# Experts' weights in transfers of 2 MB instead of 1 MB, into ten slots instead of twenty-one, with features and inner units in the order of the runs

## The chip, the core and the metric

The kernel runs on one core of one Trainium2 chip. The core has five engines: PE (TensorE, the matmuls; PEld is its loading of the stationary operand), DVE (VectorE), ACT (ScalarE), POOL (GpSimd) and SP (SyncE, which in this kernel only issues transfers), and 16 DMA engines that share its transfers out. The metric is the time of the whole kernel on the device, in microseconds (us), as the median of several runs.

## What is computed

The reference is one block of a diffusion transformer, for 256 latent tokens of 1024 features and 256 context tokens, in fp32. The first half (an adaLN-modulated norm, a combined projection, retention and latent attention side by side, a gated merge and an output projection) is not touched by the change. The second half is a mixture of 32 experts, of which each token gets four:

```python
h2 = modulate(rms_norm(x, norm2_g), m_lat[3], m_lat[4])
logits = h2 @ router_w + router_b                    # 32 experts
top_val, top_idx = lax.top_k(logits, 4)
gates = softmax(top_val)
...
gu = xb @ w_gu[e] + b_gu[e]                          # 1024 x 2048
gate, up = gu[:, :1024], gu[:, 1024:]
gate = minimum(gate, 7.0); up = clip(up, -7.0, 7.0)
glu = gate * sigmoid(1.702 * gate)
y = ((up + 1.0) * glu) @ w_down[e] + b_down[e]       # 1024 x 1024
...
x = x + m_lat[5] * sum over the token's experts of gate * y
out = rms_norm(x, final_norm_g)
```

An expert's weights are 8 MB (w_gu) and 4 MB (w_down), so that 32 experts are 402.7 MB (million bytes) that have to be read once. The sums over features (in w_gu) and over inner units (in w_down) may be taken in any order, as long as both factors of a product follow the same one.

## The kernel before

**The first half** is written as a list of steps (`step`), each with a weight that is loaded some steps ahead by SP (`load`, L258, tiles `w_...`), split into two parts by ACT (L267) and DVE (L268), and multiplied in three passes on PE (L276 to L278). It ends with the output projection (`w_out`, eight loads of 512 KB), the residual, and the transposes of the new x for the router (`x2_rows`, through the helper at L147).

**The experts** run one after the other, two sharing one gather. A block of up to 64 tokens per expert is enough for these inputs, and the code for more tokens (`overflow`) is branched over. For each expert PE does:

- the biases, `gu_bias` (L1307), once per expert, which begin the banks of the first layer
- `gate_up` (L1444): eight blocks k of 128 features; the stationary operand is xg, the gathered, transposed tokens (128 features x 64 slots), the moving one the weights, 512 columns at a time. In its middle stands `combine` (L1426), which adds the expert before to its tokens
- on DVE and ACT the clamps and the gating (L1448 to L1452), which end in `up`: 64 slots on each half of the partitions, 512 inner units each
- `slot_rows` (L1415) and `gather` (L1393) for the experts to come: 24 matmuls per expert, whose stationary operands are 128 features of the tokens in three bfloat16 parts (tiles `acc_m` and `x`)
- `hidden`: four transposes of `up` (L147), ACT copies them to hT
- `down` (L1473): eight blocks f of 128 inner units, hT stationary and the weights moving. `weigh` follows on DVE and ACT. The last expert's is done by columns (L1595), so that the last norm can begin earlier.

**The weights** come in 384 transfers of 1 MB, all issued by SP, in the order of their use: per expert eight by `load_gu` (L1067: 128 rows of 2048, a row of 8 KB to each partition), then four by `load_down` (L1072: rows p and p + 128 of 256, two runs of 4 KB to a partition). The very last one is issued in two halves (`load_last`). They go to a ring of 21 slots of 8 KB per partition. The slots come into being as the first half gives back its memory: `add_ring` opens some, with one load each. `open_first` has 2, which are reserved from the start, `RINGS = 4, 3, 9, 1` the others, and two more take the place of the output projection's operands (`halves`). From then on a slot is loaded again when PE has done its last matmul on it. SP works its transfers off in order, at most eight of them in flight.

Of the kernel before, what the change touches and what calls it, by code (L numbers as in the profile page):

```python
# [20 lines left out]
T = 256  # L21
# [8 lines left out]
RINGS = 4, 3, 9, 1  # L30
# [29 lines left out]
def hybrid_block(ctx: ExitStack, tc: tile.TileContext, A, out, dbg=None):  # L60
# [27 lines left out]
    first = [enter(ctx, f"first{i}", side="right", reuse_waits="tile") for i in range(2)]  # L88
# [12 lines left out]
    crow = sp.tile([16, 128], F32, name="crow")  # L101
    grow = sp.tile([21, 128], F32, name="grow")
# [9 lines left out]
    nc.gpsimd.dma_start(grow[8:16], A["norm2_g"].rearrange("o (k p) -> (o k) p", p=128))  # L112
    nc.gpsimd.dma_start(grow[16:19], A["mla_q_norm_g"].rearrange("o (k p) -> (o k) p", p=128))
    nc.gpsimd.dma_start(grow[19:21], A["mla_kv_norm_g"].rearrange("o (k p) -> (o k) p", p=128))
# [34 lines left out]
    def rsqrt(p, ss, n, mul, name="rs_y"):  # L149
        """(ss * mul + EPS) ** -0.5"""  # L150
# [34 lines left out]
    g1c, g2c, qgc, kvgc = cols[:, 0:8], cols[:, 8:16], cols[:, 16:19], cols[:, 19:21]  # L185

    def gain_cols():
        rp = pt_()
        transpose(rp[:, 0:21], grow)
        nc.vector.tensor_copy(cols, rp[:, 0:21])  # L190

    # ada[32 g + r]: (shift, scale) of columns 0.., then 512..; then gate, gate, shift, shift; scale, scale, gate, gate
# [4 lines left out]
    # The work up to the output projection is a list of steps; those with weights get them loaded and split ahead.  # L197
# [6 lines left out]
    def run_steps():  # L204
# [40 lines left out]
    def load(src, r0, nk, pieces, raw=False):  # L245
        """rows r0.. (nk blocks of 128), the columns of all pieces side by side"""
# [72 lines left out]
    def ada_step(q, k):  # L319
        """columns 2048 (q + 1).. of the modulation, rows 128 k.."""  # L320
# [59 lines left out]
    def project(pieces, jobs, kks, mid=None, at=None):  # L380
        """jobs: (bank, part of it, token tile, first column, end column of the loaded ones, starts its bank)"""
# [20 lines left out]
    def matmul2(names, wname, r0, c0, src, k0, first, last):  # L402
        """256 rows from r0 of a weight matrix, 512 columns, against the blocks k0.. of transposed tokens"""
# [195 lines left out]
    def q_up(quad, kks):  # L599
        """queries of four heads: the transposed parts without positions, and the rotated ones"""  # L600
# [42 lines left out]
    def q_rot(pair):  # L643
        """the rotated parts: the high parts in the upper 64 rows, what they lack in the lower"""
# [34 lines left out]
    def scores(pair):  # L679
        """softmax of both heads, for both token tiles"""  # L680
# [83 lines left out]
    def log_decay():  # L764
        """log_sigmoid(r) = min(r, 0) - log1p(exp(-|r|)), log1p(e) = 2 atanh(e / (2 + e))"""
# [41 lines left out]
    def open_ret():  # L807
# [13 lines left out]
        # the normed tokens as rows, in the two parts  # L821
# [14 lines left out]
    def r_rows():  # L836
        """the normed, gated output of a head, transposed and split"""
# [110 lines left out]
    # scores against the normed tokens first, then the value columns of w_in  # L948
# [33 lines left out]
    def gate_ret_out(c):  # L982
        """the heads so far and the other branch, gated; the gate stays for the last head"""
# [10 lines left out]
    for h in range(RH):  # L994
# [25 lines left out]
        if h == RH - 1:  # L1020
            step(lambda: open_first())
# [43 lines left out]
    def load_gu(wgu, k):  # L1065
        w = wtile()
        nc.sync.dma_start(w, wgu[128 * k:128 * k + 128])  # L1067
        return w

    def load_down(wdn, j):  # L1070
        w = wtile()
        nc.sync.dma_start(w.rearrange("p (r n) -> p r n", r=2),  # L1072
                          wdn[256 * j:256 * j + 256].rearrange("(r p) n -> p r n", p=128))
        return w

    def load_last(wdn, j):
        w = wtile()
        for r in range(2):
            nc.sync.dma_start(w[:, 1024 * r:1024 * r + 1024], wdn[256 * j + 128 * r:256 * j + 128 * r + 128])
        return w  # L1080
# [3 lines left out]
            for f, name, n in ((load_gu, "exp_w_gu", 8), (load_down, "exp_w_down", 4)) for i in range(n)]  # L1084
    todo[-1] = load_last, *todo[-1][1:]
# [5 lines left out]
    def take(f, src, i):  # L1091
        """the next weights of the experts in their order, or others"""
# [584 lines left out]
```

## Time and profile before

| what | before |
|---|---|
| time, 3 runs | 1523.48, 1525.47, 1526.0 us; median 1525.47 us |
| profiled execution, first to last instruction | 1526.6 us |
| busy: PE, PEld, DVE, ACT | 94%, 50%, 40%, 23% |
| mean granted TensorE clock | 0.991 of full |
| bytes that DMA moved | 492.42 MB, mean 323 GB/s |
| first matmul on an expert's weights | 582.27 us |
| first such matmul of the last expert | 1481.86 us |

The profile is of one execution, and it comes as a page and as views of its trace. In the page's rows of 40 slices each number stands for 38.2 us. A group of instructions is a row: line, engine, operation, tiles written and read, count, then busy time and mean ns of one, then the idle time of the engine before them and what ended it. In a timeline the first number is the start in us, the second how long the stretch took, and the brackets hold the idle time before it and its cause. In the windows view each stretch has its length, the busy time (and instructions) of PE, PEld, DVE, ACT and POOL, the granted clock, the mean busy share of the 16 DMA engines (it can pass 1 a little, since packets at the edges are counted whole) and GB/s.

### The profile page before, as it was taken

The page shows a single profiled execution, that of the slowest core. Times are in us where ns is not written, and L with a number is a line of the kernel's source. Part 1 is how long each engine was busy: PE and PEld are TensorE (multiplying, and loading weights), DVE is VectorE, ACT ScalarE, POOL GpSimd, SP SyncE. Part 2 cuts the span into 40 slices and gives each one's busy share as a digit, 9 for nine tenths or more (in the row PEclk, how much of TensorE's full clock was granted, in tenths as well). Part 3 has the DMA queues.
Part 4 walks back from the last instruction along what each step waited for, and adds up shares of the span by engine and source line. Part 5 has one row for each costly group of instructions (what it writes and reads, how often), then busy time and mean ns, then how long its engine had stood idle before and what let it go on. Part 6 is the DMA issues. An engine that isn't in the chain of part 4 may idle for free.

```text
span 1526.6 us, 19528 instructions
## 1 busy us (share of the span) xinstructions
PE 1427.5 (94%) x7977; PEld 761.8 (50%) x7977; DVE 614.0 (40%) x1079; ACT 345.9 (23%) x606; POOL 77.6 (5%) x98
## 2 busy tenths in 40 slices
PE   8999999999999998999999998899898889898985
PEld 4676787888888774333333333333332333233323
DVE  4486645556476573332322332222322232223223
ACT  4354533444344341010110101100110011001001
POOL 3100040101010020000000000000000000000000
PEclk9999999999999999999999999999999999999998
DMA  8635364354548877999999999999999999999994
GB/s 314 200 108 169 135 207 134 111 173 130 170 120 287 314 288 282 415 415 418 416 415 417 416 417 415 416 418 417 415 417 416 417 415 418 417 415 416 417 417 183
DMA packets 117658, 492.42 MB, mean 323 GB/s; under 512 B 9488, under 2 KB 19789, under 8 KB 84793
## 3 DMA queue, kind: packets, MB, share of 16 engines
q1 hardware_dynamic: 116616, 489.23, 82.1%
q0 software_dynamic: 544, 1.21, 0.3%
q8 instruction: 64, 1.05, 0.3%
q10 hardware_dynamic: 400, 0.66, 0.1%
q14 instruction: 34, 0.27, 0.0%
HBM read 490.02 MB, written 1.05 MB: 322 GB/s over the span
## 4 chain that ended last, share of the span: by engine, by line
PE 61%; DMA 29%; DVE 7%; issue 1%; ACT 1%; POOL 0%; DVEq 0%; ACTq 0%; SPq 0%
DMA w<-in_exp_w_gu_dram 26%; PE ps L1444 12%; PE ps L276 9%; PE ps L277 9%; PE ps L278 9%; PE ps L1473 9%; PE ps L1307 4%; PE ps L147 3%; DMA w<-in_exp_w_down_dram 3%; DVE up L1452 1%; DVE up L1450 1%; PE ps L299 1%; PE ps L330 1%; DVE up L1451 1%; PE ps L287 1%
## 5 line engine op out<-in xcount | busy, mean ns | idle before, releaser
L1444 PE MATMUL ps<-w,xg 128*64 128x512 f32 x2048 | 473.6, 599 | 44.8 <-DMA w<-in_exp_w_gu_dram 43.7
L1444 PEld LDWEIGHTS ps<-w,xg 128*64 128x64 f32 x2048 | 134.3, 136 | 361.2 <-issue 215.5
L1473 PE MATMUL ps<-w,ga 128*64 128x512 f32 x992 | 218.7, 593 | 0.0
L268 DVE TENSOR_TENSOR ws<-w,ws 128x1024 fp32r<-128x1024 f32 (+2 forms) x114 | 138.9, 1225 | 74.1 <-ACT ws L267 71.4
L1433 DVE SCALAR_TENSOR_TENSOR x<-ps,gate,x 128x512 f32<-128x512 f32 x124 | 84.5, 744 | 200.2 <-PE ps L1426 200.2
L1473 PEld LDWEIGHTS ps<-w,ga 128*64 128x64 f32 x992 | 71.6, 138 | 142.6 <-issue 140.8
L267 ACT ACTIVATE ws<-w 128x1024 fp32r<-128x1024 f32 (+2 forms) x114 | 116.9, 1027 | 96.9 <-PE ps L278 82.1
L1449 ACT ACTIVATE ps<-ga 128x512 f32<-128x512 f32 x32 | 19.3, 602 | 492.7 <-DVE ga L1448 492.7
L1482 DVE TENSOR_TENSOR ps<-ps,gate 128x512 f32<-128x512 f32 (+1 forms) x33 | 22.6, 684 | 267.3 <-PE ps L1473 258.4
L277 PE MATMUL ps<-ws,hh 128*128 128x512 f32 (+3 forms) x304 | 108.8, 358 | 3.7 <-DVE ws L268 3.7
L276 PE MATMUL ps<-ws,hh 128*128 128x512 f32 (+3 forms) x304 | 109.3, 360 | 0.0
L278 PE MATMUL ps<-ws,hl 128*128 128x512 f32 (+3 forms) x304 | 108.7, 357 | 0.4 <-DVE hl L375 0.4
L1448 DVE TENSOR_SCALAR ga<-ps 128x512 f32<-128x512 f32 x32 | 22.1, 692 | 169.5 <-PE ps L1444 169.5
L272 ACT ACTIVATE up<-ps 128x512 fp32r<-128x512 f32 (+1 forms) x33 | 19.3, 584 | 260.7 <-DVE ps L1482 260.6
L277 PEld LDWEIGHTS ps<-ws,hh 128*128 128x128 f32 x304 | 57.1, 188 | 13.2 <-DVE ws L268 5.0
L276 PEld LDWEIGHTS ps<-ws,hh 128*128 128x128 f32 x304 | 57.1, 188 | 12.8 <-issue 4.4
L1307 PE MATMUL ps<-bgu,ident 128*64 128x512 f32 x256 | 63.2, 615 | 0.0
L278 PEld LDWEIGHTS ps<-ws,hl 128*128 128x128 f32 x304 | 57.1, 188 | 8.2 <-DVE hl L375 0.7
L147 PE MATMUL ps<-ident,up 128*128 128x128 f32 x128 | 20.9, 286 | 22.9 <-DVE up L1452 22.9
L1393 PE MATMUL ps<-oh,acc_m 128*128 128x128 bf16 x512 | 40.5, 223 | 0.0
L278 PE MATMUL ps<-ath,htl 128*128 128x256 f32 x128 | 35.8, 280 | 0.0
L276 PE MATMUL ps<-ath,hth 128*128 128x256 f32 x128 | 35.7, 279 | 0.0
(381 smaller groups left out, 1794.4 us busy)
## 6 DMA issues: line engine op xcount, KB each, us to landing
w<-in_exp_w_gu_dram SPq DMA_DIRECT2D x256, 1024.0 KB, 19.9
w<-in_exp_w_down_dram SPq DMA_DIRECT2D x127, 1024.0 KB, 20.0
w<-in_ada_w_dram SPq DMA_DIRECT2D x48, 512.0 KB, 4.5
w<-in_w_in_dram SPq DMA_DIRECT2D x48, 512.0 KB, 4.3
w<-in_w_in_dram SPq DMA_DIRECT2D x32, 256.0 KB, 5.2
w<-in_w_branch_ret_dram SPq DMA_DIRECT2D x16, 512.0 KB, 4.6
w<-in_w_branch_mla_dram SPq DMA_DIRECT2D x8, 512.0 KB, 5.1
w<-in_w_out_dram SPq DMA_DIRECT2D x8, 512.0 KB, 11.9
```

Of the source, the lines that this page charges most:

```text
L147: nc.tensor.transpose(dst, src, ident[:n, :n])
L267: nc.scalar.activation(hi[:, :n], src, AF.Copy)
L268: nc.vector.tensor_tensor(lo[:, :n], src, hi[:, :n].bitcast(F32), op=OP.subtract)
L276: nc.tensor.matmul(ps, a[0], b[0], start=start, stop=False, skip_group_check=True)
L277: nc.tensor.matmul(ps, a[0], b[1], start=False, stop=False, skip_group_check=True)
L278: nc.tensor.matmul(ps, a[1], b[0], start=False, stop=stop, skip_group_check=True)
L1307: nc.tensor.matmul(ps[64 * h:64 * h + 64], pick_row(c // 512).to_broadcast([128, CAP]), bgu, start=True, stop=False, skip_group_check=True)
L1393: nc.tensor.matmul(ps[:, i, :w], part[:, t, ks], rhs, start=(t + p + i == 0), stop=(t + p == 3), skip_group_check=True)
L1433: nc.vector.scalar_tensor_tensor(a, pss[h], g[:, t:t + 1], a, op0=OP.mult, op1=OP.add)
L1444: nc.tensor.matmul(ps[64 * h:64 * h + 64], xg[k // 4][:, k % 4, sl], w[:, c:c + 512], start=False, stop=(k == KD - 1), skip_group_check=True)
L1473: nc.tensor.matmul(py[64 * h:64 * h + 64], hT[f], w[:, 1024 * r + 512 * h:1024 * r + 512 * h + 512], start=(f == 0), stop=(f == KD - 1))
L1482: nc.vector.tensor_tensor(py, py, gate2[:, cs], op=OP.mult)
```

## The change

Each transfer has 2 MB: `load_gu` takes 256 rows, two neighbouring ones to a partition, and `load_down` 512 rows, four neighbouring ones, so that a partition gets one run of 16 KB from both. The ring has ten slots of 16 KB per partition (`RINGS = 3, 1, 4, 1` and one in the place of both `halves`, which are opened together); the two reserved slots are given up to the first three, and no expert's weights are loaded before these. The six transfers of the last expert come in parts: the first four in two of 1 MB (runs of 8 KB), the last two in four of 512 KB (runs of 4 KB).

With that, a block of features is every second one of 256 (`pairs`), and a block of inner units every fourth of 512 (`fours`). All that meets the weights follows: the gather's stationary operands, the transposes of `up` and of x for the router, of the adaLN rows, the rows of the router's weights, and the second norm's gain, which gets a load of its own (`grow2`), two small transposes and a copy. The core of the diff:

```diff
-RINGS = 4, 3, 9, 1
+RINGS = 3, 1, 4, 1
...
+    def pairs(row, j):
+        return row.rearrange("s (j p r) -> s j r p", j=j, r=2)
...
-    def load_gu(wgu, k):
+    def load_gu(wgu, j):
         w = wtile()
-        nc.sync.dma_start(w, wgu[128 * k:128 * k + 128])
+        nc.sync.dma_start(w, wgu[256 * j:256 * j + 256].rearrange("(p r) n -> p (r n)", r=2))
         return w

     def load_down(wdn, j):
         w = wtile()
-        nc.sync.dma_start(w.rearrange("p (r n) -> p r n", r=2),
-                          wdn[256 * j:256 * j + 256].rearrange("(r p) n -> p r n", p=128))
+        nc.sync.dma_start(w, wdn[512 * j:512 * j + 512].rearrange("(p r) n -> p (r n)", r=4))
         return w

-    def load_last(wdn, j):
+    def in_parts(src, j, nr, n):
         w = wtile()
-        for r in range(2):
-            nc.sync.dma_start(w[:, 1024 * r:1024 * r + 1024], wdn[256 * j + 128 * r:256 * j + 128 * r + 128])
+        rows = src[128 * nr * j:128 * nr * j + 128 * nr].rearrange("(p r) n -> p r n", r=nr)
+        for r in range(nr):
+            nc.sync.dma_start(w[:, n * r:n * r + n], rows[:, r])
         return w
...
     def wtile():
         r = slots[nring[0] % len(slots)]
         nring[0] += 1
-        return r.tile([128, 2048], F32, name="w")
+        return r.tile([128, 4096], F32, name="w")
...
-    def open_first():
-        add_ring(0, others=first)
-
     def open_ring():
         hps.close()
+        firsts.close()
         add_ring(RINGS[0], side="right")
...
-                transpose(ps[:, j], x[:, t, cs][:, 128 * j:128 * j + 128])
+                transpose(ps[:, j], pairs(x[:, t, cs], 2)[:, j // 2, j % 2])
...
-                    nc.tensor.matmul(ps[:, i, :w], part[:, t, ks], rhs, start=(t + p + i == 0), stop=(t + p == 3),
+                    k = 4 * k4 + i
+                    nc.tensor.matmul(ps[:, i, :w], pairs(part[:, t], 4)[:, k // 2, k % 2], rhs, start=(t + p + i == 0), stop=(t + p == 3),
...
-            w = take(load_gu, wgu, k)
+            if k % 2 == 0:
+                w = take(load_gu, wgu, k // 2)
             for ps, h, c in halves:
+                c += 2048 * (k % 2)
...
+        fours = up.rearrange("s (p r) -> s r p", r=4)
         for c in range(4):
-            transpose(ps[:, c], up[:, 128 * c:128 * c + 128])
+            transpose(ps[:, c], fours[:, c])
```

On SP, at the end of the first half, the experts' first weights stand among the last loads of the output projection (`in_w_out`). Before, behind two that were issued earlier, this was the order:

```order
L258 DMA w_4609<-in_w_out_dram 128x2x512
L1067 DMA w<-in_exp_w_gu_dram 128x2048 x4
L258 DMA w_4717<-in_w_out_dram 128x2x512
L258 DMA w_4763<-in_w_out_dram 128x2x512
L258 DMA w_4824<-in_w_out_dram 128x2x512
L258 DMA w_4841<-in_w_out_dram 128x2x512
L1067 DMA w<-in_exp_w_gu_dram 128x2048 x2
L1072 DMA w<-in_exp_w_down_dram 128x2x1024
L258 DMA w_4963<-in_w_out_dram 128x2x512
L258 DMA w_4980<-in_w_out_dram 128x2x512
L1072 DMA w<-in_exp_w_down_dram 128x2x1024 x3
L1067 DMA w<-in_exp_w_gu_dram 128x2048 x8
```

After, at the same place on SP:

```order
L267 DMA w_4609<-in_w_out_dram 128x2x512
L1075 DMA w<-in_exp_w_gu_dram 128x4096 x3
L267 DMA w_4714<-in_w_out_dram 128x2x512
L267 DMA w_4760<-in_w_out_dram 128x2x512
L267 DMA w_4821<-in_w_out_dram 128x2x512
L267 DMA w_4838<-in_w_out_dram 128x2x512
L1075 DMA w<-in_exp_w_gu_dram 128x4096
L267 DMA w_4950<-in_w_out_dram 128x2x512
L267 DMA w_4967<-in_w_out_dram 128x2x512
L1080 DMA w<-in_exp_w_down_dram 128x4096 x2
L1075 DMA w<-in_exp_w_gu_dram 128x4096 x4
```

Three transfers of 2 MB (6 MB) stand ahead of four `w_out` loads where four of 1 MB stood, one of 2 MB ahead of the last two instead of three of 1 MB, and the two that were issued earlier are gone.

On PE, where the experts' weights are waited for, DMAHW0 to DMAHW7 are the semaphores on which transfers report. Before, in the middle of the experts:

```order
L1444 MATMUL ps<-w,xg 64x512 [waits DMAHW3_49]
L1444 MATMUL ps<-w,xg 64x512 x3
L1444 MATMUL ps<-w,xg 64x512 [waits DMAHW4_49]
L1444 MATMUL ps<-w,xg 64x512 x3
L1444 MATMUL ps<-w,xg 64x512 [waits DMAHW5_49]
L1444 MATMUL ps<-w,xg 64x512 x3
```

After, at the start of an expert's first layer (behind the last product of the expert before it):

```order
L1482 MATMUL ps<-w,ga 64x512 x7
L1451 MATMUL ps<-w,xg 64x512 [waits DMAHW3_49]
L1451 MATMUL ps<-w,xg 64x512 x7
L1451 MATMUL ps<-w,xg 64x512 [waits DMAHW4_49]
L1451 MATMUL ps<-w,xg 64x512 x7
L1431 MATMUL ps<-up,ct 128x512 [waits Activation_49]
```

PE now waits once for two blocks of features, eight matmuls, and no longer for each.

More of the change, by code (lines that the diff above doesn't have):

```diff
@@ L87, in hybrid_block @@
     accp = enter(ctx, "accp", side="right")
-    first = [enter(ctx, f"first{i}", side="right", reuse_waits="tile") for i in range(2)]
+    firsts = ExitStack()
+    first = [enter(firsts, f"first{i}", side="right", reuse_waits="tile") for i in range(2)]
     hps = ExitStack()
@@ L101, in hybrid_block @@
     crow = sp.tile([16, 128], F32, name="crow")
-    grow = sp.tile([21, 128], F32, name="grow")
+    grow = sp.tile([13, 128], F32, name="grow")
+    grow2 = sp.tile([4, 256], F32, name="grow2")
     x0 = sp.tile([128, 4, D], F32, name="x0")
@@ L184, in hybrid_block @@
     cols = fk.tile([128, 21], F32, name="cols")
-    g1c, g2c, qgc, kvgc = cols[:, 0:8], cols[:, 8:16], cols[:, 16:19], cols[:, 19:21]
+    g1c, qgc, kvgc, g2c = cols[:, 0:8], cols[:, 8:11], cols[:, 11:13], cols[:, 13:21]
+    def pairs(row, j):
+        return row.rearrange("s (j p r) -> s j r p", j=j, r=2)
     def gain_cols():
         rp = pt_()
-        transpose(rp[:, 0:21], grow)
-        nc.vector.tensor_copy(cols, rp[:, 0:21])
+        transpose(rp[:, 0:13], grow)
+        for r in range(2):
+            transpose(rp[:, 16 + 4 * r:20 + 4 * r], pairs(grow2, 1)[:, 0, r])
+        nc.vector.tensor_copy(cols[:, 0:13], rp[:, 0:13])
+        nc.vector.tensor_copy(g2c.rearrange("p (j r) -> p r j", r=2), rp[:, 16:24].rearrange("p (r j) -> p r j", r=2))
     ada0 = sp.tile([128, 512], F32, name="ada0")
@@ L1019, in hybrid_block @@
         step(ret_scores)
-        if h == RH - 1:
-            step(lambda: open_first())
         ada_step(1, 2 * h + 1)
@@ L1083, in hybrid_block @@
     todo = [(f, A[name][0, e], i) for e in range(E)
-            for f, name, n in ((load_gu, "exp_w_gu", 8), (load_down, "exp_w_down", 4)) for i in range(n)]
-    todo[-1] = load_last, *todo[-1][1:]
+            for f, name, n in ((load_gu, "exp_w_gu", 4), (load_down, "exp_w_down", 2)) for i in range(n)]
+    todo[-6:] = [((lambda s, j: in_parts(s, j, 2, 2048)) if f is load_gu else (lambda s, j: in_parts(s, j, 4, 1024)), src, i)
+                 for f, src, i in todo[-6:]]
     def fetch():
@@ L1121, in open_late @@
         O["rw"] = late.tile([128, KD, E], F32, name="ct")
-        nc.gpsimd.dma_start(O["rw"], A["router_w"][0].rearrange("(k p) e -> p k e", p=128))
+        nc.gpsimd.dma_start(O["rw"].rearrange("p (j r) e -> p j r e", r=2),
+                            A["router_w"][0].rearrange("(j p r) e -> p j r e", p=128, r=2))
         O["rbias"] = late.tile([128, E], F32, name="rbias")
@@ L1133, in close_early @@
         add_ring(RINGS[1], side="right")
-        open_half(0)
+        halves.append(enter(ctx, "halves", side="right", reuse_waits="tile"))
+        both = halves[0].tile([128, 2, 2, KD // 2, T], F32R, name="w")
+        for q in range(2):
+            O["m", q] = both[:, q, 0], both[:, q, 1]
     halves = []
-    def open_half(q):
-        halves.append(enter(ctx, f"half{q}", side="right", reuse_waits="tile"))
-        both = halves[q].tile([128, 2, KD // 2, T], F32R, name="w")
-        O["m", q] = both[:, 0], both[:, 1]
     def open_out():
@@ L1145, in open_out @@
         dump("merged", M["acc"])
-        open_half(1)
         O["tmp"] = enter(tmps, "tmp", side="right", reuse_waits="tile")
@@ L1391, in gather @@
                 for i in range(4):
-                    ks = slice(512 * k4 + 128 * i, 512 * k4 + 128 * i + 128)
-                    nc.tensor.matmul(ps[:, i, :w], part[:, t, ks], rhs, start=(t + p + i == 0), stop=(t + p == 3),
+                    k = 4 * k4 + i
+                    nc.tensor.matmul(ps[:, i, :w], pairs(part[:, t], 4)[:, k // 2, k % 2], rhs, start=(t + p + i == 0), stop=(t + p == 3),
                                      skip_group_check=True)
@@ L1467, in down @@
         py = pt_()
-        for j in range(4):
+        for j in range(2):
             w = take(load_down, wdn, j)
-            for r in range(2):
-                f = 2 * j + r
+            for r in range(4):
+                f = 4 * j + r
                 for h in range(2):
@@ L1558, in wide @@
     def wide():
-        return wtile().rearrange("p (t n) -> p t n", t=2)
+        return wtile()[:, :2048].rearrange("p (t n) -> p t n", t=2)
     def store(t, h, xf):
@@ L1588, in hybrid_block @@
     pys = [pt_((128, 256)) for _ in range(2)]
-    for j in range(4):
+    for j in range(2):
         w = take(load_down, None, j)
-        for f in (2 * j, 2 * j + 1):
+        for f in range(4 * j, 4 * j + 4):
             for c in range(2):
                 for h in range(2):
-                    o = 1024 * (f % 2) + 512 * h + 256 * c
+                    o = 1024 * (f % 4) + 512 * h + 256 * c
                     nc.tensor.matmul(pys[c][64 * h:64 * h + 64], hT[f], w[:, o:o + 256],
```

10 lines of the change are left out of this document (5 added, 5 removed).

## The prediction

> **What bounds the kernel now.** I read the page first: the bytes that the DMA engines moved, the chain that ended last and the DMA issues.
>
> ```profile
> GB/s 314 200 108 169 135 207 134 111 173 130 170 120 287 314 288 282 415 415 418 416 415 417 416 417 415 416 418 417 415 417 416 417 415 418 417 415 416 417 417 183
> DMA w<-in_exp_w_gu_dram 26%; PE ps L1444 12%; PE ps L276 9%; PE ps L277 9%; PE ps L278 9%; PE ps L1473 9%; PE ps L1307 4%; PE ps L147 3%; DMA w<-in_exp_w_down_dram 3%; DVE up L1452 1%; DVE up L1450 1%; PE ps L299 1%; PE ps L330 1%; DVE up L
> w<-in_exp_w_gu_dram SPq DMA_DIRECT2D x256, 1024.0 KB, 19.9
> w<-in_exp_w_down_dram SPq DMA_DIRECT2D x127, 1024.0 KB, 20.0
> w<-in_w_out_dram SPq DMA_DIRECT2D x8, 512.0 KB, 11.9
> ```
>
> From slice 17 (611 us) to the last but one the rate stands at 415 to 418 GB/s: the experts' 402.7 MB stream at a constant rate for 57% of the span. PE is 94% busy over the span, so the question is which of the two ends later. The timeline of PE answers it, first early in the experts:
>
> ```profile
> 655.35 1.94 PE L1307 MATMUL ps<-bgu,ident 128*64 128x512 f32 x8
> 663.98 7.04 PE L1444 MATMUL ps<-w,xg 128*64 128x512 f32 x32
> 681.69 0.66 PE L147 MATMUL ps<-ident,up 128*128 128x128 f32 x4 [0.97 <-DVE up L1452]
> 682.28 1.94 PE L1307 MATMUL ps<-bgu,ident 128*64 128x512 f32 x8
> ```
>
> L1307 comes once per expert, so an expert takes 682.28 - 655.35 = 26.93 us here, and no DMA ends a wait: PE (with DVE's short chain) is the limit. Then late:
>
> ```profile
> 1016.61 1.94 PE L1307 MATMUL ps<-bgu,ident 128*64 128x512 f32 x8
> 1029.22 1.94 PE L1444 MATMUL ps<-w,xg 128*64 128x512 f32 x8 [0.38 <-DMA w<-in_exp_w_gu_dram]
> 1031.70 1.94 PE L1444 MATMUL ps<-w,xg 128*64 128x512 f32 x8 [0.54 <-DMA w<-in_exp_w_gu_dram]
> 1039.16 1.94 PE L1444 MATMUL ps<-w,xg 128*64 128x512 f32 x8 [0.55 <-DMA w<-in_exp_w_gu_dram]
> 1041.68 1.94 PE L1444 MATMUL ps<-w,xg 128*64 128x512 f32 x8 [0.58 <-DMA w<-in_exp_w_gu_dram]
> 1046.52 1.94 PE L1307 MATMUL ps<-bgu,ident 128*64 128x512 f32 x8
> ...
> 1441.39 1.94 PE L1307 MATMUL ps<-bgu,ident 128*64 128x512 f32 x8
> ```
>
> Here each block waits for its weights, an expert takes 29.91 us, and from 1046.52 to 1441.39 are 13 experts of 30.37 us. PE eats the ring's stock in the first half (some 3 us per expert faster than DMA fills it) and is then tied to DMA. So the time of the end is: when the stream starts, plus bytes over rate, plus a tail. Only the rate, the start and the tail can change the time.
>
> **The rate.** L1067 (gate and up) moves runs of 8 KB, L1072 (down) runs of 4 KB. In the windows view the stretch 1008:1016 holds mostly 4 KB packets and 1020:1034 mostly 8 KB ones; the share of 16 engines is 1.01 or more in both, so both are the engines' own pace.
>
> ```profile
> 1008.00:1016.00 8.00, 5.90 (x48) 2.55 (x44) 3.04 (x6) 0.90 (x2) 0.00 (x0) 1.00 1.02 408
> 1020.00:1034.00 14.00, 13.09 (x62) 4.09 (x60) 1.39 (x2) 0.60 (x1) 0.00 (x0) 1.00 1.01 420
> ```
>
> The DMA view of the same two stretches gives their packets:
>
> ```profile
> DMA packets 807, 3.26 MB, mean 408 GB/s; under 512 B 50, under 2 KB 50, under 8 KB 767
> ```
>
> ```profile
> DMA packets 809, 5.87 MB, mean 420 GB/s; under 512 B 87, under 2 KB 87, under 8 KB 99
> ```
>
> Per engine a 4 KB packet takes 4096 x 16 / 408 = 160.6 ns and an 8 KB one 8192 x 16 / 420 = 312.1 ns. The second 4 KB cost 151.5 ns, so 9.1 ns belong to the packet and not to its bytes. I continue the line: a 16 KB packet takes 312.1 + 2 x 151.5 = 615.1 ns, or 426 GB/s. An expert before is 64 packets of each kind per engine, 64 x (160.6 + 312.1) = 30.25 us (the timeline has 30.37); after, 48 of 16 KB, 48 x 615.1 = 29.52 us: **-0.73 us per expert**. In the steady part 176 transfers of 2 MB run (192 in all, less the 10 that fill the ring and the 6 that come in parts), 176 / 6 = 29.33 experts: **-21.4 us**. The two rates are uncertain by some 2 GB/s: with 410 and 422 the line's slope falls and the gain goes towards -26, with 408 and 418 it is -18.
>
> The Trainium skill ("DMA: Bandwidth & Descriptors", Why small descriptors are slow) names a fixed cost of about three cycles per packet, and advises packing descriptors only at 256 B or less; by that, nothing worth having would be left between 4 and 16 KB. The same page's ceiling (Where 436 GB/s comes from) is 435.2 GB/s; an estimate from it is 402.7 MB / 435.2 = 925 us for all weights, 43 us under what 416 GB/s takes, and that is the most that any packet size could bring. The trace's 408 against 420 speaks against "nothing left"; what that would give is rival A.
>
> **The start.** These are the windows around the first expert, PE's first matmuls on its weights, and SP's last loads into new slots and first ones into slots that are used again (584.25 and later):
>
> ```profile
> 572.00:576.00 4.00, 0.00 (x0) 0.00 (x0) 3.82 (x11) 0.41 (x2) 2.94 (x4) 0.80 0.55 223
> 576.00:580.00 4.00, 3.84 (x39) 3.67 (x39) 2.08 (x9) 0.81 (x3) 0.76 (x4) 0.50 0.00 0
> 580.00:584.00 4.00, 4.00 (x39) 2.79 (x38) 2.84 (x8) 1.76 (x4) 0.00 (x0) 0.85 0.00 0
> 584.00:588.00 4.00, 4.00 (x22) 1.39 (x20) 0.00 (x0) 0.00 (x0) 0.00 (x0) 1.00 0.69 211
> 588.00:592.00 4.00, 4.00 (x22) 1.30 (x20) 0.00 (x0) 0.38 (x1) 0.00 (x0) 1.00 0.95 334
> ```
>
> ```profile
> 582.27 7.09 PE L1444 MATMUL ps<-w,xg 128*64 128x512 f32 x32
> ```
>
> ```profile
> 543.35 19.32 SPq L1067 DMA_DIRECT2D w<-in_exp_w_gu_dram  x8
> 569.78 0.38 SPq L1072 DMA_DIRECT2D w<-in_exp_w_down_dram  x1
> 584.25 3.80 SPq L1072 DMA_DIRECT2D w<-in_exp_w_down_dram  x3
> 589.40 2.58 SPq L1067 DMA_DIRECT2D w<-in_exp_w_gu_dram  x2
> ```
>
> The ring is full at 576, DMA stands still, and starts again when PE gives back the first slot, at 584.25; PE then frees 1 MB in each 7.09 / 4 = 1.77 us. After the change the ring holds 20 MB instead of 21, and the first slot comes back after 2 MB, one such step later, about 586.0; each load then brings 2 MB. The stream starts 1.7 us later, and 1.05 MB more is left to move (1.05 / 0.416 = 2.5 us): **+4.2 us**. PE has stock at that time and doesn't feel it, but the stream never stops again before the end, so I count it whole.
>
> That all ten slots are full by 582 rests on the fill: the last slots open with the same events as before (six of them, from 543.35 to 569.78), and they now take 2 MB each. From 543 to 582 DMA has 39 us, or 16 MB at 416 GB/s, for these 12.6 MB: nothing. Were the last one late, PE would reach it only some 30 us after its first matmul (nine slots of 3.5 us).
>
> The three 2 MB loads now stand ahead of four of the w_out loads on SP, at the place of four of 1 MB. That is 2 MB, 4.9 us later for these; but the third w_out weight is split at 527.55, after a wait for PE:
>
> ```profile
> 495.26 11.81 SPq L258 DMA_DIRECT2D w<-in_w_out_dram  x4
> ```
>
> ```profile
> 527.55 1.06 ACT L267 ACTIVATE ws<-w 128x1024 fp32r<-128x1024 f32 x1 [5.65 <-PE ps L278]
> ```
>
> Issued at 495.26 and landing 11.9 us later (row of the page above), it lies there 20 us ahead. Nothing; without that cover it would be at most +4.9 us.
>
> **What PE pays.** The features and inner units now follow the runs, so that the operand that PE loads for the gather (24 per expert, bf16, every second element), for the hidden transposes (4, fp32, every fourth) and for 16 transposes of x2 (fp32, every second) is read with a stride. Before, all were dense:
>
> ```profile
> L1393 PEld LDWEIGHTS <-acc_m 128*128 128x128 bf16 x512 | 31.9, 100 | 2.2 <-issue 0.8
> L147 PEld LDWEIGHTS ps<-ident,up 128*128 128x128 f32 x128 | 13.4, 140 | 28.2 <-DVE up L1452 25.4 <-issue 2.4 <-PE ps L1378 0.4
> ```
>
> No row has a strided one, so I bound it: below by nothing (weight loads run beside matmuls), above by each load taking four times as long, an end far off that the rows only allow, which is 24 x 300 + 4 x 420 ns = 8.9 us per expert. PE has room: without DMA waits it would do 31 experts of 26.85 us (the early pace) after 582.27 and begin the last at 1414.6, DMA's forecast puts that at about 1465; 50 us over 31 experts are 1.6 us each that PE may lose for nothing. (1465 is 1481.86, its start in the tail's rows below, less 21.4 and plus 4.2.) I take +0.2 us per expert, nearer to the dense rows, which are the only ones there are, hidden by that room, and **+0.7 us** where nothing hides it: 16 transposes of x2 ahead of the first expert and the last expert's four, 20 loads a quarter longer, 20 x 35 ns. The adds of a tiny load, two transposes and a copy for the second norm's gain lie under the adaLN loads: nothing.
>
> The Trainium skill ("SBUF — State Buffer", the note on cachelines) says that SBUF is read in lines of 16 bytes and that a read needs two hits in a line to run at full rate. A stride of 4 bytes (gather) keeps four, of 8 bytes (x2) two; the hidden transposes step 16 bytes, a new line for each element. By that rule the four loads are slow, the others aren't, and the sum would stay as it is, since 4 x 420 ns is about the room above; no run yet shows it.
>
> **The tail.** The last gate/up waits and the last product:
>
> ```profile
> 1481.86 7.04 PE L1444 MATMUL ps<-w,xg 128*64 128x512 f32 x32
> 1494.25 1.94 PE L1444 MATMUL ps<-w,xg 128*64 128x512 f32 x8 [0.57 <-DMA w<-in_exp_w_gu_dram]
> 1496.77 1.94 PE L1444 MATMUL ps<-w,xg 128*64 128x512 f32 x8 [0.58 <-DMA w<-in_exp_w_gu_dram]
> 1503.06 7.13 PE L1595 MATMUL ps<-w,ga 128*64 128x256 f32 x64
> ```
>
> The last expert's transfers come in parts of 1 MB (8 KB runs) and 512 KB (4 KB runs), as fine as before, so that the tail after the last landing keeps its length: nothing. Had it stayed at 2 MB, the last block would begin up to 2.5 us later.
>
> **Sum.** 1526.6 - 21.4 + 4.2 + 0.7 = 1510.1 us for this execution's span. The median of the runs, 1525.47, is 1.1 us below that span, so I forecast **1509.0 us**. Its own range, from the gains of 18 to 26 us and 0 to +3 us at the start's and PE's edges, is 1504 to 1516.
>
> **The rivals.**
>
> A. *The per-byte rate doesn't improve beyond 8 KB.* Then a 16 KB run costs two of 8 KB, 624.2 ns, an expert 29.96 us, and only the down weights gain: 0.29 x 29.33 = -8.5, +4.9 as above, sum -3.6: 1521.9. For it: only two sizes carry the line, and the difference of 12 GB/s is read from stretches of 8 and 14 us. Against it: the 9.1 ns per packet have no reason to stop at 8 KB. That the engines cut a 16 KB run in two (the change not doing what it says) gives the same number. 13%.
>
> B. *Slower: strided operands make PE the bound.* Place: the 28 weight loads per expert. The gather of one expert in the early stretch of PE's timeline:
>
> ```profile
> 679.21 0.62 PE L1393 MATMUL ps<-oh,acc_m 128*128 128x128 bf16 x8
> 680.33 0.39 PE L1393 MATMUL ps<-oh,x 128*128 128x128 bf16 x4
> ```
>
> Price: beyond the 1.6 us of room each further 0.1 us per expert costs 3.1 us. The last expert would begin as late as today, 1481.86, at (1481.86 - 582.27) / 31 = 29.02 us per expert, 2.2 us more than now; from there it is slower. At 2.6 us more (each of the 28 loads 93 ns longer, and all of it in the way) it begins at 582.3 + 31 x 29.45 = 1495.2, 13.4 us later than today: 1539. For it: a gather load's 100 ns is longer than the 63 ns in which its matmuls follow each other (24 in 1.51 us, from 679.21 to 680.72), so PE is already at the pace of its loads there. Against: at half that pace the gather would take 1.5 us more, which is under the room. 5%.
>
> C. *Slower or even: long runs go slower than the line.* The gain equals the +4.9 us at 30.25 - 4.9 / 29.33 = 30.08 us per expert, 627 ns per packet; from there it is slower. At 640 ns an expert is 30.72 us, and the sum 0.47 x 29.33 + 4.9 = +18.7: 1544. For it: the two sizes that carry the line are both below. Against: 4 and 8 KB both run at a share of 1.01 or more, with no sign of a limit but bytes and packets. 5%.
>
> D. *Better.* Should an engine's pace at 16 KB lose all of a packet's cost (606 ns, 29.09 us per expert), it is -34.0 + 4.9: 1496.4. 5%.
>
> The forecast keeps 72%. **The numbers:** the range goes from 1500 (between the forecast's lower end and D) to 1524 (A with 2 us of further loss); outside are B, C, most of D. 0.2%, about what a measurement of this kernel tells from no change, is 3.1 us: even is 1522.4 to 1528.5. Faster: the forecast, D and A's half below 1522.4, less a little for unknown losses, 0.82; even: A's other half and that little, 0.08; slower: B and C, 0.10.
>
> **What would show it.** Right: the late rate at 424 to 428 GB/s in place of 416; the bias matmuls that come once per expert 29.5 us apart late; the first load into a used slot at about 586; waits of the blocks for DMA still there late, one of some 1.5 us per 2 MB in place of 0.55 per 1 MB; the weight loads of the gather still near 100 ns. Wrong: late waits for DMA gone (B), a late rate of 420 or less (A or C), or PE idle for DMA in the first five experts (the fill).

## The result, and the profile after

The changed kernel takes 1507.82 us (median of 4 runs, 1507.01 to 1508.17) against 1525.05 us (4 runs, 1523.48 to 1526.0) for the kernel before: a ratio of 0.9882, 95% interval [0.9859, 0.9905]. The forecast was 1509.0 us, in a range of 1500 to 1524. The profiled execution spans 1506.0 us; its mean granted clock is 0.993.

These are the lines of its page that answer to those shown of before: the rate in 40 slices (37.7 us each), the packets, the chain and the issues.

```profile
GB/s 319 203 109 144 140 227 108 128 192 112 182 126 210 352 166 369 426 426 427 426 428 425 429 425 427 428 425 429 426 427 426 428 427 428 426 427 427 427 422 178
DMA packets 75046, 492.38 MB, mean 327 GB/s; under 512 B 6563, under 2 KB 16860, under 8 KB 50120
DMA w<-in_exp_w_gu_dram 25%; DMA w<-in_exp_w_down_dram 13%; PE ps L1451 11%; PE ps L285 9%; PE ps L287 9%; PE ps L286 9%; PE ps L1482 5%; PE ps L149 3%; PE ps L1312 1%; PE ps L308 1%; PE ps L339 1%; PE ps L296 1%; PE ps L1431 1%; PE ps L437
w<-in_exp_w_gu_dram SPq DMA_DIRECT2D x124, 2048.0 KB, 39.1
w<-in_exp_w_down_dram SPq DMA_DIRECT2D x62, 2048.0 KB, 39.1
```

The rate in the steady part went from 415 to 418 up to 425 to 429 GB/s, and the chain still leads through the experts' weights (25% and 13% of the span): DMA is the bound as before, at a better pace. A transfer takes 39.1 us from issue to landing where it took 19.9 or 20.0: twice the bytes, the same eight in flight.

The DMA view of the stretch 1000 to 1400 of the changed kernel puts a number on the pace:

```profile
DMA packets 11730, 170.82 MB, mean 427 GB/s; under 512 B 1302, under 2 KB 1302, under 8 KB 1302
```

Apart from 1302 tiny packets all are long ones, of 16 KB, so the runs were not cut in two. At 427 GB/s each takes 16384 x 16 / 427 = 614 ns on its engine, where the line through 4 and 8 KB had 615.1. PE's timeline shows what an expert takes by its bias matmuls (L1312), early and then late:

```profile
653.20 1.94 PE L1312 MATMUL ps<-bgu,ident 128*64 128x512 f32 x8
680.21 1.94 PE L1312 MATMUL ps<-bgu,ident 128*64 128x512 f32 x8
...
1009.27 1.94 PE L1312 MATMUL ps<-bgu,ident 128*64 128x512 f32 x8
1022.30 3.65 PE L1451 MATMUL ps<-w,xg 128*64 128x512 f32 x16 [0.80 <-DMA w<-in_exp_w_gu_dram]
1032.09 3.65 PE L1451 MATMUL ps<-w,xg 128*64 128x512 f32 x16 [1.24 <-DMA w<-in_exp_w_gu_dram]
...
1423.66 1.94 PE L1312 MATMUL ps<-bgu,ident 128*64 128x512 f32 x8
```

Early it is 27.01 us, 0.08 more than before. Late it is (1423.66 - 1009.27) / 14 = 29.60 us. The prediction took 30.37 for before, from 13 experts; over 14, as here, it is (1441.39 - 1016.61) / 14 = 30.34 (both rows stand in the prediction). So an expert takes 0.74 us less, where the prediction had 0.73. PE's waits for weights are still there, fewer and longer: 0.80 and 1.24 us in place of four of about 0.5, a little under the 1.5 that were expected.

At the start of the experts, this is PE's first matmul on their weights, SP's first loads into used slots, and the DMA share around them:

```profile
579.83 4.51 PE L1451 MATMUL ps<-w,xg 128*64 128x512 f32 x20
```

```profile
583.52 3.76 SPq L1080 DMA_DIRECT2D w<-in_exp_w_down_dram  x2
590.91 3.76 SPq L1075 DMA_DIRECT2D w<-in_exp_w_gu_dram  x2
```

```profile
576.00:580.00 4.00, 4.00 (x53) 3.90 (x52) 2.13 (x8) 0.91 (x4) 0.76 (x4) 0.73 0.97 414
580.00:584.00 4.00, 4.00 (x20) 1.33 (x20) 1.48 (x5) 1.15 (x3) 0.00 (x0) 1.00 0.06 23
584.00:588.00 4.00, 4.00 (x20) 1.26 (x18) 0.00 (x0) 0.38 (x1) 0.00 (x0) 1.00 0.90 287
```

The first slot comes back 3.69 us after the first matmul, where it took 1.98: 1.7 us later, as forecast. The ring of 20 MB is full at about 580 (the DMA share falls from 0.97 to 0.06), just in time. But the first matmul itself stands 2.44 us earlier than before, which no step of the prediction has; the last experiments deal with that.

And the tail:

```profile
1476.45 1.94 PE L1451 MATMUL ps<-w,xg 128*64 128x512 f32 x8 [0.53 <-DMA w<-in_exp_w_gu_dram]
1482.83 7.13 PE L1604 MATMUL ps<-w,ga 128*64 128x256 f32 x64
```

From the last block's start to the end of the span are 1506.0 - 1476.45 = 29.55 us, before 1526.6 - 1496.77 = 29.83.

### The profile page after: what moved, and what is told of

Its sections match the earlier page's. It is cut to its first block, busy times and chain, and to the rows that moved or that the text cites. A ratio compares the mean times of both kernels' runs of the same rounds, so it can differ in the third digit from the quotient of the medians.

```text
span 1506.0 us, 19151 instructions
## 1 busy us (share of the span) xinstructions
PE 1414.9 (94%) x7979; PEld 771.2 (51%) x7979; DVE 613.6 (41%) x1080; ACT 345.8 (23%) x606; POOL 77.0 (5%) x98
## 3 DMA queue, kind: packets, MB, share of 16 engines
q8 instruction: 64, 1.05, 0.3%
HBM read 490.02 MB, written 1.05 MB: 326 GB/s over the span
## 4 chain that ended last, share of the span: by engine, by line
PE 55%; DMA 38%; DVE 5%; ACT 1%; issue 1%; POOL 0%; ACTq 0%; DVEq 0%; SPq 0%
DMA w<-in_exp_w_gu_dram 25%; DMA w<-in_exp_w_down_dram 13%; PE ps L1451 11%; PE ps L285 9%; PE ps L287 9%; PE ps L286 9%; PE ps L1482 5%; PE ps L149 3%; PE ps L1312 1%; PE ps L308 1%; PE ps L339 1%; PE ps L296 1%; PE ps L1431 1%; PE ps L437 1%; DVE up L1459 1%
## 5 line engine op out<-in xcount | busy, mean ns | idle before, releaser
L1451 PE MATMUL ps<-w,xg 128*64 128x512 f32 x2048 | 460.1, 596 | 38.1 <-DMA w<-in_exp_w_gu_dram 36.0
L1451 PEld LDWEIGHTS ps<-w,xg 128*64 128x64 f32 x2048 | 140.6, 137 | 336.0 <-issue 251.6
L1455 DVE TENSOR_SCALAR ga<-ps 128x512 f32<-128x512 f32 x32 | 22.1, 691 | 162.4 <-PE ps L1451 162.4
L286 PEld LDWEIGHTS ps<-ws,hh 128*128 128x128 f32 x304 | 57.1, 188 | 12.8 <-DVE ws L277 4.6
L1312 PE MATMUL ps<-bgu,ident 128*64 128x512 f32 x256 | 62.0, 605 | 0.0
L1471 ACT ACTIVATE ga<-ps 128x512 f32<-128x512 f32 x32 | 19.1, 597 | 74.5 <-PE ps L149 74.5
## 6 DMA issues: line engine op xcount, KB each, us to landing
w<-in_exp_w_gu_dram SPq DMA_DIRECT2D x124, 2048.0 KB, 39.1
w<-in_exp_w_down_dram SPq DMA_DIRECT2D x62, 2048.0 KB, 39.1
```

Of the source, the lines that this page charges most:

```text
L286: nc.tensor.matmul(ps, a[0], b[1], start=False, stop=False, skip_group_check=True)
L1312: nc.tensor.matmul(ps[64 * h:64 * h + 64], pick_row(c // 512).to_broadcast([128, CAP]), bgu, start=True, stop=False, skip_group_check=True)
L1451: nc.tensor.matmul(ps[64 * h:64 * h + 64], xg[k // 4][:, k % 4, sl], w[:, c:c + 512], start=False, stop=(k == KD - 1), skip_group_check=True)
```

## The experiments

The theory is the prediction's: a packet costs a fixed 9 ns beside its bytes, so that the length of the runs sets DMA's rate; DMA sets the end; the ring's stock and the moment when it is first refilled are paid in full. (What the 9 ns consist of, no run shows: in all of them the length of a packet and the length of a run in memory go together.) Its rivals: the size of the transfer makes the gain, not the runs; nothing is left to gain beyond 8 KB; strided operands cost PE time that counts.

**2 MB transfers of the old runs.** The changed kernel, with rows 128 apart:

```diff
-        nc.sync.dma_start(w, wgu[256 * j:256 * j + 256].rearrange("(p r) n -> p (r n)", r=2))
+        nc.sync.dma_start(w.rearrange("p (r n) -> p r n", r=2), wgu[256 * j:256 * j + 256].rearrange("(r p) n -> p r n", p=128))
...
-        nc.sync.dma_start(w, wdn[512 * j:512 * j + 512].rearrange("(p r) n -> p (r n)", r=4))
+        nc.sync.dma_start(w.rearrange("p (r n) -> p r n", r=4), wdn[512 * j:512 * j + 512].rearrange("(r p) n -> p r n", p=128))
...
-        return row.rearrange("s (j p r) -> s j r p", j=j, r=2)
+        return row.rearrange("s (j r p) -> s j r p", j=j, r=2)
```

and the same for `fours`, the last parts and the router's rows.

> 2 MB transfers and ten slots as after the change, but each made of the old runs: two rows 128 apart (8 KB runs) for gate and up, four rows 128 apart (4 KB runs) for down; all operands dense on PE again. If the length of the runs makes the gain: an expert late takes 64 x (160.6 + 312.1) ns = 30.25 us again, 29.33 experts x 0.73 = 21.4 us more than the changed kernel, about 1529. If the size of the transfer makes it (fewer transfers, fewer waits), the time stays at 1508 within 3.

Measured: 1528.37 us (1527.65 to 1529.35), a ratio to before of 1.0019, [1.001, 1.0028]. Its late pace, again by the bias matmuls, 14 experts apart:

```profile
1019.55 1.94 PE L1312 MATMUL ps<-bgu,ident 128*64 128x512 f32 x8
...
1444.19 1.94 PE L1312 MATMUL ps<-bgu,ident 128*64 128x512 f32 x8
```

That is 30.33 us per expert, the pace of before (30.34). So the whole gain lies in the runs: 1528.37 - 1507.82 = 20.6 us, 21.4 forecast. Transfers of 2 MB by themselves are a small loss: 3.1 us against the 1525.27 us of the kernel before beside it. Forecast for the later refill and the smaller stock were +4.2; this run doesn't divide the 3.1 between the two.

**Short runs for the down weights only.** The edit of the second `dma_start` above and of `fours`; gate and up keep 16 KB.

> As the changed kernel, but the down weights come in four rows 128 apart (4 KB runs) per partition, and the transposes of up are dense; gate and up keep 16 KB runs. By runs: 64 x 160.6 - 16 x 615.1 ns = 0.44 us per expert, 29.33 experts, +12.8: 1520.6. By the size of the transfers alone: 1508. If only the first step from 4 KB up counts and 8 to 16 KB gives nothing, the whole gain goes: about 1525.

Measured: 1519.05 us (1518.83 to 1519.25), ratio 0.9957, [0.994, 0.9974]. The step of the down weights from 4 to 16 KB is worth 11.2 us (12.8 forecast), that of the gate and up weights from 8 to 16 KB the other 9.3 (8.5 forecast). The gain does not stop at 8 KB.

**Runs of 8 KB for down, in the kernel before.** With 1 MB transfers and 21 slots:

```diff
-        nc.sync.dma_start(w.rearrange("p (r n) -> p r n", r=2),
-                          wdn[256 * j:256 * j + 256].rearrange("(r p) n -> p r n", p=128))
+        nc.sync.dma_start(w, wdn[256 * j:256 * j + 256].rearrange("(p r) n -> p (r n)", r=2))
...
+        twos = up.rearrange("s (c p r) -> s c r p", c=2, r=2)
         for c in range(4):
-            transpose(ps[:, c], up[:, 128 * c:128 * c + 128])
+            transpose(ps[:, c], twos[:, c // 2, c % 2])
```

> The kernel before, with 1 MB transfers and 21 slots, but the down weights with two neighbouring rows per partition (runs of 8 KB in place of two of 4 KB) and the transposes of up with a stride of two. By runs: 64 x 160.6 - 32 x 312.1 ns = 0.29 us per expert, 30 experts behind the fill, -8.8: 1516.3 against 1525.05. By the size of the transfers: no change, 1525.

Measured: 1516.89 us (1516.6 to 1517.65), ratio 0.9944, [0.9927, 0.9961]: 8.4 us less than the 1525.27 us before, without a change to the transfers' size (8.8 forecast). All weights now come in runs of 8 KB, and over 400 us the windows view has the 420 GB/s that the prediction read for them from a stretch of 14 us:

```profile
1000.00:1400.00 400.00, 362.89 (x1967) 130.56 (x1964) 109.81 (x181) 39.32 (x87) 0.00 (x0) 1.00 1.01 420
```

**Nine slots instead of ten.** `RINGS = 3, 1, 3, 1`, and one less in the order in which the late ones are filled.

> The changed kernel with nine slots (18 MB) in place of ten. If what is not in by the first expert is simply left to move at 427 GB/s: 2.1 MB / 0.427 = +4.9 us, 1512.7. If the stock doesn't matter because PE has enough of it: 1508. If nine slots are too few for the eight transfers in flight, DMA stands still at times and it is over 1515.

Measured: 1512.06 us (1511.72 to 1512.41), ratio 0.9904, [0.9886, 0.9923]: 4.2 us more than the changed kernel's 1507.82, and 5.9 more than the 1506.16 us that it took when both were run side by side (the last experiment). From the first expert to the end its profiled execution takes 931.1 us, 5.0 more than the changed kernel's 926.2. The 4.9 us forecast lie between: each MB that isn't in when PE begins is paid at DMA's rate at the end, though PE has stock for some 340 us after that (its first wait for weights comes at 917.21, its first expert at 579.37).

**Whole transfers at the end.** The two lines that put the last six transfers in parts are removed.

> The changed kernel without the parts: the last six transfers are whole ones of 2 MB. The last gate and up block then can't begin before all its 2 MB are there, 1.8 us later (half a block of 3.6 us is left to do after the last byte), and the down product waits for its last 2 MB: +2 to +4, about 1510. If the tail is set by the last down weights only and these land as before: 1508.

Measured: 1509.12 us (1507.69 to 1509.97), ratio 0.99, [0.9884, 0.9917]. This is 1.3 us above the changed kernel and within what the runs tell apart. Its last gate and up block, in PE's timeline, begins 2 us earlier than the last half block of the changed kernel, and ends at nearly the same time (1478.1 and 1478.4):

```profile
1474.48 3.65 PE L1449 MATMUL ps<-w,xg 128*64 128x512 f32 x16 [1.23 <-DMA w<-in_exp_w_gu_dram]
1481.06 0.70 PE L149 MATMUL ps<-ident,up 128*128 128x128 f32 x4
1482.58 7.13 PE L1602 MATMUL ps<-w,ga 128*64 128x256 f32 x64
```

Its first expert begins at 578.46, though, 1.4 us earlier, so that from there to the end it is 1.3 us slower. So the parts are worth some 1.3 us, under the 2 to 4 expected, and no run tells it from nothing with certainty.

**More work on PE.** Some of an expert's four bias matmuls are done again (each starts its bank anew, so that the sums stay the same):

```diff
-        for ps, h, c in halves:
+        for ps, h, c in halves[:2] + halves:
             nc.tensor.matmul(ps[64 * h:64 * h + 64], pick_row(c // 512).to_broadcast([128, CAP]), bgu,
```

> The changed kernel with two of the four bias matmuls of an expert done twice (+0.9 us of PE work per expert, same result). If DMA bounds the end and PE has (1462.1 - 579.8) / 31 - 26.9 = 1.5 us per expert to spare, nothing changes: 1508 within 2. If PE's work still counts beside DMA, up to 31 x 0.9 = 28 us more: 1536.

Measured: 1510.03 us (1508.92 to 1511.37), ratio 0.9902, [0.9886, 0.9919]: 2.2 us more than the changed kernel, just over the 2 us of the expectation, and far from 28. The profiled executions are 3.5 us apart (1509.5 and 1506.0), of which 0.6 is a later first expert. The rest can be placed. The first loads wait a little longer for their slots; the windows of this kernel show DMA short of work once, here with the same stretch of the changed kernel as the last line:

```profile
600.00:604.00 4.00, 4.00 (x22) 1.30 (x20) 0.00 (x0) 0.00 (x0) 0.00 (x0) 1.00 1.00 430
604.00:608.00 4.00, 4.00 (x21) 1.19 (x18) 0.00 (x0) 0.00 (x0) 0.00 (x0) 1.00 0.93 315
...
604.00:608.00 4.00, 4.00 (x38) 1.98 (x34) 0.72 (x2) 0.60 (x1) 0.00 (x0) 1.00 0.98 397
```

From the first expert (580.43) to the last wait of the last but one (1448.95) are 868.5 us, 1.6 more than in the changed kernel (1446.74 - 579.83 = 866.9). And at the end, where PE no longer waits for weights, its own work counts; from that last wait to the end are 1.3 us more than in the changed kernel:

```profile
1455.02 0.72 PE L149 MATMUL ps<-ident,up 128*128 128x128 f32 x4 [2.31 <-DVE up L1459]
1455.67 4.49 PE L1312 MATMUL ps<-bgu,ident 128*64 128x512 f32 x12
1466.86 7.04 PE L1451 MATMUL ps<-w,xg 128*64 128x512 f32 x32
1474.95 7.09 PE L1451 MATMUL ps<-w,xg 128*64 128x512 f32 x32
```

The last expert's blocks (from 1466.86) wait for no weights here. So the room of 1.5 us per expert is there in the long middle, and not at its two ends.

The same with six more, `halves[:2] + halves + halves`:

> The changed kernel with six bias matmuls more per expert (+2.65 us of PE work). By the room of 1.5 us: PE becomes the bound and the time grows by (2.65 - 1.5) x 31 = 36 us: 1543. If the room were 2.65 or more: 1508.

Measured: 1540.44 us (1539.58 to 1541.3, 2 runs), ratio 1.0104, [1.0084, 1.0124], and 32.6 us more than the changed kernel (36 forecast). Here no block waits for DMA, and late as early an expert takes 29.4 and 29.6 us in turn:

```profile
1012.04 4.51 PE L1312 MATMUL ps<-bgu,ident 128*64 128x512 f32 x20
1023.25 7.04 PE L1451 MATMUL ps<-w,xg 128*64 128x512 f32 x32
1031.34 7.09 PE L1451 MATMUL ps<-w,xg 128*64 128x512 f32 x32
1041.64 3.65 PE L1312 MATMUL ps<-bgu,ident 128*64 128x512 f32 x16
```

The point from which PE decides lies near where it was worked out: PE's mean of 29.5 us per expert is 2.6 more than the changed kernel's early pace; with 1.5 us of room, 1.1 x 31 = 34 us are lost.

**Other strides.** The gather's operand takes every eighth feature, the transposes of `up` are dense:

```diff
-                    nc.tensor.matmul(ps[:, i, :w], pairs(part[:, t], 4)[:, k // 2, k % 2], rhs, start=(t + p + i == 0), stop=(t + p == 3),
+                    nc.tensor.matmul(ps[:, i, :w], part[:, t].rearrange("s (p r) -> s r p", r=8)[:, k], rhs, start=(t + p + i == 0), stop=(t + p == 3),
...
-        fours = up.rearrange("s (p r) -> s r p", r=4)
+        fours = up.rearrange("s (r p) -> s r p", r=4)
```

> The changed kernel with other strides on PE: the gather's bf16 operand takes every eighth feature (16 bytes from one element to the next, where the change has 4), and the transposes of up are dense. Features and inner units then don't fit their weights; the amount of work is the same. If a new 16-byte line for each element slows a load, the 24 gather loads per expert go from 99 ns to 150 or more, and the early pace from 26.9 to up to 28 us per expert; the loads of up go from 209 back to 140 ns. The time stays at 1508 within 2 in either case, since PE has 1.5 us per expert to spare. If only fp32 operands pay for a stride, the gather stays at 99 ns.

This kernel leaves out the match of features and inner units with their weights, so its output isn't the block's; only its times are of use.

Measured: 1507.76 us (1507.13 to 1508.18), the changed kernel's time. The groups of PE's weight loads, of the changed kernel:

```profile
L1398 PEld LDWEIGHTS <-acc_m 128*128 128x128 bf16 x512 | 31.5, 99 | 2.2 <-issue 0.8
L149 PEld LDWEIGHTS ps<-ident,up 128*128 128x128 f32 x128 | 17.8, 208 | 28.2 <-DVE up L1459 25.4 <-issue 2.4 <-PE ps L1383 0.4
L149 PEld LDWEIGHTS ps<-ident,x 128*128 128x128 f32 x48 | 5.8, 164 | 2.1 <-issue 1.7 <-DVE x L1212 0.3
```

and of this one:

```profile
L1398 PEld LDWEIGHTS <-acc_m 128*128 128x128 bf16 x512 | 37.6, 148 | 2.2 <-issue 0.8
L149 PEld LDWEIGHTS ps<-ident,up 128*128 128x128 f32 x128 | 13.4, 140 | 22.4 <-DVE up L1459 19.6 <-issue 2.4 <-PE ps L1383 0.4
```

A bf16 load with 4 bytes from element to element costs what a dense one does (99 against 100 ns), with 16 bytes 148. An fp32 load with 16 bytes costs 208 against 140. In the kernel before with down weights in pairs the transposes of `up` step 8 bytes, and they cost as much:

```profile
L147 PEld LDWEIGHTS ps<-ident,up 128*128 128x128 f32 x128 | 17.8, 209 | 28.2 <-DVE up L1451 25.4 <-issue 2.4 <-PE ps L1377 0.4
```

None of it is slower than by half, and the early pace shows which of it PE feels. Of this kernel, and as the last line of the changed one:

```profile
653.65 1.94 PE L1312 MATMUL ps<-bgu,ident 128*64 128x512 f32 x8
679.99 0.66 PE L149 MATMUL ps<-ident,up 128*128 128x128 f32 x4 [0.77 <-DVE up L1459]
680.57 1.94 PE L1312 MATMUL ps<-bgu,ident 128*64 128x512 f32 x8
...
679.53 0.75 PE L149 MATMUL ps<-ident,up 128*128 128x128 f32 x4 [0.97 <-DVE up L1459]
```

An expert takes 680.57 - 653.65 = 26.92 us here, the pace of before, though each of the gather's 24 loads is 49 ns longer: the gather stands ahead of a wait for DVE, which is shorter by as much as the gather is longer (0.77 in place of 0.97 us). The four transposes stand behind that wait, and their 0.66 us became 0.75 in the changed kernel. That is its 0.08 us per expert. It also answers what spoke for rival B, that PE runs the gather at the pace of its loads: with loads longer by half the gather takes 0.2 us more, and all of it is hidden.

**Where the earlier start came from.** In the profiled execution of before, PE waits 0.81 us ahead of the sums with the router's weights (L1177), and then its clock is down:

```profile
519.04 1.29 PE L147 MATMUL ps<-ident,r 128*128 128x128 f32 x8 [0.92 <-DVE r L976]
521.14 1.94 PE L1177 MATMUL ps<-ct,mod 128*128 128x32 f32 x16 [0.81 <-DVE atl L273]
```

```profile
524.00:528.00 4.00, 4.00 (x13) 3.13 (x13) 0.84 (x1) 0.45 (x1) 0.00 (x0) 0.67 0.40 153
```

The profile puts the wait down to DVE, but DVE's instruction has nothing to do with these operands (it writes `atl`, which L278 uses later). The router's weights (`ct`, loaded by POOL) were issued at 510.6 and landed 10.4 us later, at 521.0; in the changed kernel they took 6.4 us. So a transfer of the experts' weights that SP issues at 509.35, just ahead of them, was the suspect. In this experiment it is held back, by the order in which three slots are filled:

```diff
-        add_ring(RINGS[1], side="right")
+        add_ring(RINGS[1], (2, 0, 1), side="right")
```

> The kernel before, but of the three slots that open together ahead of the last two w_out loads the one that comes free last is loaded first, so that no expert's weights go out between 509 and 515 us. If the router's weights were held up by these transfers (landing 10.4 us after their issue before, 6.4 after the change), they land at about 517, PE starts its sums on them without a wait, its clock stays up, and the first expert begins 2.4 us earlier, at 579.9: 1522.6. If the earlier start of the changed kernel has another cause (the runs of 256 bytes in the router's own load), it stays at 582.3 and 1525.

Measured: the router's weights land 6.6 us after their issue, PE doesn't wait for them, its clock stays at 1.00, and the first expert begins at 577.85; but the time is 1524.23 us (median of 11 runs; ten took 1523.28 to 1525.67 us, one 3650.47) with a ratio of 0.999, [0.9981, 0.9999], a gain of 1 us, not 2.4 or the 4.4 by which the start moved in the profile. So most executions of before can't have had that wait. Two more profiles of the kernel before itself were to show it.

> The kernel before, once more, for the profile of another execution. If the router's weights are always held up behind the experts' weights of 509 us, they land some 10.4 us after their issue, the first expert begins at 582.3, and the earlier start (by 2.4 us) belongs to the change. If that was a matter of one execution, as the 8.0 us of the kernel with down weights in pairs hint, they land in 8 us or less and the first expert begins at about 579.8.

> The same again, a third execution of the kernel before: 582.3 if the wait is the kernel's, about 579.8 if it was one execution's.

Measured: one run each, 1524.61 and 1525.15 us. The router's weights land after 8.1 and 8.2 us, PE doesn't wait for them in either, and the first expert begins at 579.06 and 579.83. From the first of the two:

```profile
520.13 1.87 PE L1177 MATMUL ps<-ct,mod 128*128 128x32 f32 x16
```

```profile
579.06 3.22 PE L1444 MATMUL ps<-w,xg 128*64 128x512 f32 x14
```

Their spans are 1522.8 and 1523.4 us, not 1526.6. So the late start is not the rule of the kernel before, but it may not be that one execution's alone: of 38 runs of before beside the experiments six took over 1527 us, and none of the ten above. Of the kernel before only three executions were profiled, so whether those six had that wait isn't shown.

**The changed kernel again**

> The changed kernel itself once more, beside the kernel before, to see how far its start at the first expert (579.83 us) and its time repeat: 1508 within 1.5, and the first expert again within 0.5 us of 579.8 if the earlier start belongs to the kernel and not to this execution.

Measured: 1506.16 us (1506.14 to 1507.82, 4 runs), ratio to before 0.9869, [0.9848, 0.9891], with the first expert at 578.66: 1.2 us off, more than the half that was expected. Between executions of one kernel the start moves by about 1 us even without that wait (before: 579.06 and 579.83).

## Why the prediction was right, step by step

- **What bounds the kernel**: right. PE's first wait for weights comes 337 us after the first expert before (919.70) and 382 us after the change (962.00), and from there DMA sets the pace; with PE work added, the change over to PE came close to the 1.5 us per expert that were worked out.
- **The rate**: right. The steady pace fell by 0.74 us per expert, 0.73 forecast. From the first refill to the last wait for gate and up weights it was 1496.77 - 584.25 = 912.5 us and is 1476.45 - 583.52 = 892.9 us; that is -19.6 with 1.05 MB more to move (2.5 us), so -22.1 for the rate, where the sum has -21.4; the kernel with the old runs has -20.6, so which way the sum errs stays open. The line through 4 and 8 KB held at 16 KB to 1 ns in 615, which rival A denied. One sum of the range is wrong: with 410 and 422 GB/s for the two sizes the gain is 0.73 x 29.33 = 21.3 us, not towards 26; it takes 408 and 422 to come to 25.
- **The start**: right in both its parts (1.7 us for the refill; each MB paid in full, by the kernel with nine slots). Together, with the old runs, they were a loss of 3.1 us, forecast 4.2.
- **w_out and the fill**: nothing, as forecast. ACT and DVE, which split the w_out weights, wait for none of these loads in the changed kernel's profile (in that of before, DVE waits for one, 1.5 us).
- **PE's strided operands**: right that nothing of it counts. Of the terms, 0.2 us per expert turned out 0.08. The 0.7 us ahead of the experts and at the tail can't be seen in the times; 20 loads longer by 70 ns, not 35, would be 1.4 us if nothing overlapped.
- **The rule of the Trainium skill** ("SBUF — State Buffer", the note on cachelines: two hits in a 16-byte line for full rate): the gather agrees with it, at 4 bytes (99 ns) and at 16 (148 ns), and so do the transposes of `up` at 16 (208 against 140 ns). fp32 with 8 bytes should still be at full rate, and is not: 209 ns, as with 16. The measurement decides.
- **The tail**: the last block to the end is as long as before (29.55 and 29.83 us). Of the up to 2.5 us that whole transfers would have cost, about 1.3 showed.
- **The sum**: 1507.82 us is nearer to 1509.0 than the terms are to what was measured. With the old runs' kernel between them the change is 3.1 - 20.6 = -17.5 us, by the terms 4.2 + 0.7 - 21.4 = -16.5: the loss was put too high and the rate's gain too, and part of that cancelled.
- **What went wrong without harm**: the sum was made against one execution of 1526.6 us, in which the first expert began 2.4 to 3.2 us later than in two others (582.27 against 579.06 and 579.83). The prediction took the 1.1 us between that span and the median for an offset between spans and times. The offset is the other way: a run's span is some 1.8 us shorter than its time (1522.8 and 1524.61, for one), so that execution took about 1528.4 us, 3 more than the median. In the forecast it falls out, since 1509.0 is the median less the terms' 16.5. The gain of the times is 17.2 us; that of the profiles without the late start is 16.8 to 19.0 (1522.8 and 1523.4 to 1506.0 and 1504.4).

## What to carry to other kernels

Where a stream of weights sets the end, read the rate by packet size from stretches in which one size dominates, take the fixed part from the difference, and continue the line: here 9 ns per packet were worth 20.6 us, 1.3% of the kernel. A larger transfer by itself gained nothing here, where eight are in flight all the time; it cost 3.1 us, by a later refill and by what no longer fits ahead, and both are paid at the end even though nobody waits for them at the start. Before a sum is made against one profiled execution, look for a wait in it that another execution might not have.

## What the runs showed of the hardware that was not expected

- Stationary operands of 128x128 on PE: bf16 99 to 100 ns dense or at 4 bytes, 148 ns at 16 bytes; fp32 140 ns dense, 208 to 209 ns at 8 and at 16 bytes.
- In the first profile of before, a wait of 0.81 us that followed one of 0.92 us was followed by a granted clock of 0.90 in the 4 us from 520 and 0.67 in the next 4. In the other 13 profiles only the first of the two waits came (0.79 us in the changed kernel, 0.93 in the two later ones of before), and the clock stayed at 1.00 in both stretches.
- A load that POOL issues (the router's weights, 128 KB) landed after 6.4 to 7.4 us in the ten profiles in which SP issues no experts' weights between 509 and 514 us, and after 8.0, 8.1, 8.2 and 10.4 us in the four in which it does. 8.2 us hurt nothing; with 10.4 PE waited 0.81 us, and the first expert began 2.4 to 3.2 us later.
